# Even mixer of a two-layer hybrid backbone: a triangular solve with two VectorE operations a step, two products on VectorE in a round of their own, and loads issued one stage earlier

## The chip, the core and the metric

The kernel runs on one core of a Trainium2 chip. The metric is the device time of one execution, in microseconds (us); lower is better. The core has TensorE (PE in the profile, its weight loads PEld), VectorE (DVE), ScalarE (ACT), GpSimd (POOL) and SyncE (SP); every engine works through its own list of instructions in the order in which they were recorded, and waits on semaphores for the others. DMAs are issued from the lists of SP, ACT and POOL.

## The reference, cut to what matters

Two layers run over 256 context rows and 256 latent rows of width 1024. The first layer is "even": an RWKV-7 time mixing in both directions, beside a small pooling mixer; the second is "odd" (attention and retention). Each is followed by a mixture of gated MLPs, and every sub-layer adds its result to the residual stream `x` times a gate (`g1` after the mixer).

```python
def step(S, inp):                       # RWKV-7, per head; state S is (value, key)
    w_t, k_t, v_t, kk_t, b_t = inp[:5]
    sa = jnp.einsum('bhvk,bhk->bhv', S, -kk_t)
    S = S * w_t[:, :, None, :] + sa[..., None] * b_t[:, :, None, :] + v_t[..., None] * k_t[:, :, None, :]
    return S, jnp.einsum('bhvk,bhk->bhv', S, inp[5])
...
x = x + g1 * y_lat                      # y_lat: the mixer's output
```

## The kernel before

The scan is worked out in chunks of 64 tokens. Within a chunk, each token's correction depends on the earlier ones through a strictly triangular matrix (64 x 64 for each head and chunk), so the kernel inverts "one plus that matrix" for all chunks first and then walks over the chunks. The work is cut into four units, (half, d): half 0 or 1 is four of the eight heads, d 0 or 1 the direction. A unit has three parts:

- `ev_prep` makes the decays (EB, EN), the decayed keys KB, the receptances and keys times the decays (RK), their transposes (tok), and the chunk matrices: products of KB and RK, masked into BA (with the diagonal) and KK (without it).
- `ev_solve` inverts the 16 x 16 diagonal blocks row by row in 15 steps, and joins blocks with small matrix products (`products`, L819). A step spreads one row of the blocks over partitions by eight small matmuls into the bank "s" (L798); VectorE multiplies it with the rows found so far (L800), sums (L802), and negates and places the sum (L803). "s" has one buffer, so the matmuls of a step wait for the L800 of the step before. X is the inverse, A16 the blocks.
- `ev_chain` walks over the eight chunks, three rounds each, and reads KK, BA, RK and tok. Its first matmul (L864) needs what the solve wrote last.

The order of the work is set by `STAGES` (eight stages) and `weave`: in one round, every generator of the stage's main list is advanced by one `yield`, in order, and then `per` pieces of the fill list (projections of the inputs, "ada" pieces that turn the conditioning into gates) follow. What is recorded in that order is the order on each engine. In this text stages are numbered from 1: stage 3 holds prep (0,1), solve (0,0) and the bonus; 4 the chain (0,0) and the solve (0,1); 5 the chain (0,1) and prep (1,0); 6 the norm, the solve (1,0) and prep (1,1); 7 the solve (1,1), the chain (1,0), the bonus and the pooling; 8 the chain (1,1) and most of the output projection. After stage 8 comes the first mixture of MLPs.

All weights come through one `Stream`: SP issues the loads in the planned order, each as soon as a buffer of its ring is given back, and holds up there otherwise. In stage 8 `ev_first` loads the residual stream `x` again (into the tiles that held the projected inputs, hT) and the gate rows `g1` (into the tiles rT and us), with DMAs from ACT's list. Its L1521 multiplies a piece of the output by a piece of g1 (tiles us and rT), and L1522 adds it to x.

Of the kernel before, what the change touches and what calls it, by code (L numbers as in the profile page):

```python
# [32 lines left out]
def shape_constants():  # L33
# [49 lines left out]
    for d in range(2):  # L83
        after = (lambda a, b: a > b) if d == 0 else (lambda a, b: a < b)
        v[f"upto{d}"] = heads & ~after(p, f)
        v[f"strict{d}"] = after(f64, p % 64)
        v[f"incl{d}"] = ~after(p % 64, f64)
        v[f"start{d}"] = (p % 16 == f16) & (f16 == (0 if d == 0 else 15))
        v[f"cross{d}"] = (p % 32 // 16 == d) & (f32 // 16 == 1 - d)
# [6 lines left out]
    for i in range(16):  # L96
        v[f"sel{i}"] = (p % 32 // 16 == f32 // 16) & (p % 16 == i)
# [112 lines left out]
class Kernel:  # L210
# [182 lines left out]
    def even(self, xp, seg):  # L393

        nc, tc, I, c = self.nc, self.tc, self.I, self.c
        with ExitStack() as st:
# [6 lines left out]
                     (("BA", 4, 64), ("KK", 4, 64), ("RK0", 2, 64), ("RK1", 2, 64), ("tok0", 128), ("tok1", 128))]  # L403
# [3 lines left out]
            with ExitStack() as s1:  # L407
# [13 lines left out]
                for n in range(5):  # L421
# [255 lines left out]
    def ev_prep(self, half, d):  # L677
# [8 lines left out]
        u["BA"], u["KK"] = (up.tile([128, 8, 4, 64], F32, name=n) for n in ("BA", "KK"))  # L686
        u["Pe"], u["PH"] = up.tile([128, 2, 8], F32, name="Pe"), up.tile([128, 2, 8, 2], F32, name="PH")
        split = lambda a: a.rearrange("p (t j i) -> p t j i", t=4, j=2)
        for q in range(2):
# [50 lines left out]
            yield  # L740
            yield
# [24 lines left out]
    def ev_solve(self, half, d):  # L766
# [19 lines left out]

        A16 = wp.tile([128, G, 16], F32, name="A16")
# [1788 lines left out]
```

## Time and profile before

| what | us |
|---|---|
| median of 3 runs | 1911.77 |
| lowest and highest of them | 1896.86 and 1915.39 |
| the profiled execution, its own time | 1917.63 |
| span of the profiled execution | 1915.9 |

The profile is of one execution. Its span runs from the first instruction to the last, and 1.7 us lie around it. Busy times of PE include matmuls that run at either clock; PEclk is the granted share of TensorE's full clock, 1.00 being 2.4 GHz and 0.50 being 1.2 GHz. On the span's axis the even mixer lies from about 58 us (after the norm and the first projections) to 570 us, the first mixture from about 570 to 1080, the odd mixer to about 1330, and the second mixture to the end.

### The profile page before, as it was taken

The page shows a single profiled execution, that of the slowest core. Times are in us where ns is not written, and L with a number is a line of the kernel's source. Part 1 is how long each engine was busy: PE and PEld are TensorE (multiplying, and loading weights), DVE is VectorE, ACT ScalarE, POOL GpSimd, SP SyncE. Part 2 cuts the span into 40 slices and gives each one's busy share as a digit, 9 for nine tenths or more (in the row PEclk, how much of TensorE's full clock was granted, in tenths as well). Part 3 has the DMA queues.
Part 4 walks back from the last instruction along what each step waited for, and adds up shares of the span by engine and source line. Part 5 has one row for each costly group of instructions (what it writes and reads, how often), then busy time and mean ns, then how long its engine had stood idle before and what let it go on. Part 6 is the DMA issues. An engine that isn't in the chain of part 4 may idle for free. (4 is left out here: it accounts for less than half of the span.)

```text
span 1915.9 us, 31673 instructions
## 1 busy us (share of the span) xinstructions
PE 1653.2 (86%) x12946; PEld 931.2 (49%) x12946; DVE 842.5 (44%) x1718; ACT 435.9 (23%) x925; POOL 161.6 (8%) x181
## 2 busy tenths in 40 slices
PE   5987999889898999999999997999978787766666
PEld 3744556545676444444444435888643333422222
DVE  2556444655358245455555458563632212212012
ACT  3432122321213211111111114453421101101101
POOL 2122001112215000000000004000100000000000
PEclk8997888889998999999999998999888989979786
DMA  9266210461433879999999972422979998999991
GB/s 315 78 210 210 89 46 23 154 204 32 163 143 132 355 288 383 405 388 389 377 395 395 374 323 74 142 86 74 378 282 414 413 383 326 414 415 414 415 411 52
DMA packets 127284, 505.80 MB, mean 264 GB/s; under 512 B 11317, under 2 KB 38945, under 8 KB 85986
## 3 DMA queue, kind: packets, MB, share of 16 engines
q1 hardware_dynamic: 119794, 490.86, 66.0%
q0 software_dynamic: 3488, 8.26, 1.3%
q10 hardware_dynamic: 3792, 3.79, 0.6%
q8 instruction: 143, 2.34, 0.5%
q14 instruction: 67, 0.55, 0.1%
HBM read 501.78 MB, written 1.10 MB: 262 GB/s over the span
## 5 line engine op out<-in xcount | busy, mean ns | idle before, releaser
L1968 PE MATMUL b<-w,ht 128*64 128x512 f32 x512 | 118.8, 604 | 8.7 <-PEq L2185 8.5
L1993 DVE TENSOR_TENSOR tmp<-b,g 128x512 f32<-128x512 f32 x128 | 87.6, 686 | 70.1 <-PE b L1991 69.2
L1947 PE MATMUL b<-w,xg 128*64 128x512 f32 x512 | 116.9, 598 | 0.0
L1947 PE MATMUL b<-w,xh 128*64 128x512 f32 x512 | 116.9, 598 | 0.0
L2275 PE MATMUL b<-w,x 128*32 128x256 f32 x1024 | 80.4, 428 | 34.2 <-DMA w<-moe_w_up 28.4
L2292 PE MATMUL b<-w,ht 128*32 128x256 f32 x1024 | 79.8, 449 | 21.8 <-ACT ht L2287 12.7
L2275 PE MATMUL b<-w,xg 128*32 128x256 f32 x1024 | 76.8, 432 | 21.6 <-DMA w<-moe_w_up 13.3
L1995 DVE TENSOR_TENSOR x<-x,tmp 128x512 f32<-128x512 f32 x124 | 90.0, 726 | 4.3
L1976 DVE TENSOR_TENSOR yl<-b,yh 64x512 fp32r<-64x512 f32 x62 | 42.7, 689 | 101.6 <-ACT yh L1975 101.6
L2280 DVE SCALAR_TENSOR_TENSOR low<-b,gs,low 64x256 f32<-64x256 f32 x32 | 15.7, 491 | 158.5 <-ACT low L2279 158.5
L1968 PEld LDWEIGHTS b<-w,ht 128*64 128x64 f32 x512 | 41.5, 138 | 84.1 <-issue 70.8
L2440 DVE COPY y<-b 32x256 f32<-32x256 f32 x62 | 25.9, 418 | 127.5 <-PE b L2292 114.2
L1951 ACT ACTIVATE low<-b 64x512 f32<-64x512 f32 x33 | 19.4, 588 | 251.9 <-PEq L2185 221.3
L2275 PEld LDWEIGHTS b<-w,x 128*32 128x32 f32 x1024 | 37.0, 120 | 75.3 <-DMA w<-moe_w_up 37.9
L1952 DVE SCALAR_TENSOR_TENSOR low<-b,gs,low 64x512 f32<-64x512 f32 x32 | 36.1, 1130 | 67.0 <-ACT low L1951 64.2
L1975 ACT CAST yh<-b 64x512 fp32r<-64x512 f32 x62 | 36.0, 581 | 129.8 <-PE b L1968 106.5
L2275 PEld LDWEIGHTS b<-w,xg 128*32 128x32 f32 x1024 | 36.7, 123 | 58.7 <-DMA w<-moe_w_up 18.4
L1947 PEld LDWEIGHTS b<-w,xh 128*64 128x64 f32 x512 | 33.9, 136 | 62.5 <-issue 62.0
L1947 PEld LDWEIGHTS b<-w,xg 128*64 128x64 f32 x512 | 33.9, 136 | 62.3 <-issue 61.3
L2279 ACT ACTIVATE low<-b 64x256 f32<-64x256 f32 (+1 forms) x36 | 14.4, 399 | 214.6 <-PEq L2485 133.1
L1991 PE MATMUL b<-yh,oht 128*128 128x512 f32 (+1 forms) x128 | 58.3, 456 | 3.2 <-DVE tmp L1993 3.2
L2292 PEld LDWEIGHTS b<-w,ht 128*32 128x32 f32 x1024 | 34.5, 124 | 52.1 <-issue 20.2
(877 smaller groups left out, 3178.3 us busy)
## 6 DMA issues: line engine op xcount, KB each, us to landing
w<-moe_w_gate SPq DMA_DIRECT2D x128, 1024.0 KB
w<-moe_w_up SPq DMA_DIRECT2D x128, 1024.0 KB
w<-moe_w_down SPq DMA_DIRECT2D x128, 1024.0 KB
w<-ada_w SPq DMA_DIRECT2D x48, 1024.0 KB
w<-od_w_in SPq DMA_DIRECT2D x12, 1024.0 KB
w<-ev_w_in SPq DMA_DIRECT2D x8, 1024.0 KB
w<-ev_w_out SPq DMA_DIRECT2D x5, 1024.0 KB
w<-od_w_out SPq DMA_DIRECT2D x4, 1024.0 KB
```

What stands on the lines that cost most here:

```text
L1947: nc.tensor.matmul(ps[64 * j:64 * j + 64], xe(k), w[j][:, k % 4], start=k == 0, stop=k == 7)
L1951: nc.scalar.activation(sg[64:128], ps[0:64], AF.Silu)
L1952: nc.vector.scalar_tensor_tensor(hs[64:128].rearrange("s k q -> s q k"), ps[64:128].rearrange("s (q k) -> s q k", k=4), gs, sg[64:128].rea ...
L1968: nc.tensor.matmul(ps[64 * j:64 * j + 64], ht[:, k], w[:, k % 2, 512 * j:512 * j + 512], start=k == 0, stop=k == 3)
L1975: nc.scalar.copy(out=yh[:, j], in_=pj)
L1976: nc.vector.tensor_tensor(yl[:, j], pj, yh[:, j].bitcast(F32), op=ALU.subtract)
L1991: nc.tensor.matmul(ps, ohT[0:n, t], y[0:n, j], start=i == 0, stop=i == len(parts) - 1)
L1993: nc.vector.tensor_tensor(tmp, ps, g2[seg[t]][:, 512 * j:512 * j + 512], op=ALU.mult)
L1995: (nc.gpsimd if j in aside else nc.vector).tensor_tensor(xs, xs, tmp, op=ALU.add)
L2275: nc.tensor.matmul(ps[groups[j]], xe(k), w[j // 2][:, k % 4, 256 * (j % 2):256 * (j % 2) + 256], start=k == 0, stop=k == 7, skip_group_che ...
L2292: nc.tensor.matmul(ps[groups[j]], ht[:, k % 2, S * (k // 2):S * (k // 2) + S], w[:, k % 2, 256 * j:256 * j + 256], start=k == 0, stop=k == ...
L2440: (nc.scalar.copy if j % 2 else nc.vector.tensor_copy)(out=out, in_=ps[groups[j]])
```

## The change

It touches the even mixer alone.

1. **Solve.** A16 now holds minus the identity as well (`subtract` of eye16), and the `sel` constants are negated, so that the reduction writes the finished row straight into X: the third VectorE operation of a step (L803) is gone. The steps' matmuls cover one more column group (the diagonal), and are recorded for two steps at once into one bank; each step still has a `yield`. X starts from a copy by ScalarE. The masking of AT (L812) goes to ScalarE and GpSimd ahead of the steps, and half of the copy into TT to ScalarE. Four `yield`s with nothing in front of them are added: two ahead of the steps, one ahead of the first block product and one after the second.
2. **Prep.** BA and KK become the halves of one tile AB, masked by one operation on 128 x 512 elements where there were two on 128 x 256. The scaling of `th` goes from VectorE to ScalarE. The two products of RK go from GpSimd to VectorE, and into the next round.
3. **Loads.** g1 is loaded by SP in stage 7, in the pooling after the bonus, and `x` by SP in stage 7 after the last projection that reads hT; `ev_first` loads nothing.

```diff
@@ ev_prep
-        u["BA"], u["KK"] = (up.tile([128, 8, 4, 64], F32, name=n) for n in ("BA", "KK"))
+        both = up.tile([128, 8, 4, 128], F32, name="AB")
+        u["BA"], u["KK"] = both[:, :, :, 0:64], both[:, :, :, 64:128]
...
-            nc.vector.tensor_scalar(th, th, self.ka[:, 0, b:b + 1], self.ka[:, 1, b:b + 1], op0=ALU.mult, op1=ALU.add)
+            nc.scalar.activation(th, th, AF.Identity, bias=self.ka[:, 1, b:b + 1], scale=self.ka[:, 0, b:b + 1])
...
-            nc.gpsimd.tensor_tensor(u["RK"][q][:, :, 1], chunks(kk), eex, op=ALU.mult)
-            nc.gpsimd.tensor_tensor(u["RK"][q][:, :, 0], chunks(rT), ein, op=ALU.mult)
...
             yield
+            nc.vector.tensor_tensor(u["RK"][q][:, :, 1], chunks(kk), eex, op=ALU.mult)
+            nc.vector.tensor_tensor(u["RK"][q][:, :, 0], chunks(rT), ein, op=ALU.mult)
             yield
...
-                    nc.vector.tensor_tensor(u["KK"][:, C, 2 * q + h], ps[:, :, 64:128],
-                                            c[f"strict{d}"][:, None, :].to_broadcast([128, 4, 64]), op=ALU.mult)
-                    nc.vector.tensor_tensor(u["BA"][:, C, 2 * q + h], ps[:, :, 0:64],
-                                            c[f"incl{d}"][:, None, :].to_broadcast([128, 4, 64]), op=ALU.mult)
+                    nc.vector.tensor_tensor(both[:, C, 2 * q + h], ps, c[f"mask{d}"][:, None, :].to_broadcast([128, 4, 128]), op=ALU.mult)
@@ ev_solve
         yield
+        nc.scalar.activation(AT[:, :, 16 - 16 * d:32 - 16 * d], AT[:, :, 16 - 16 * d:32 - 16 * d], AF.Copy, scale=c["subcol"][:, d:d + 1])
+        nc.gpsimd.memset(AT[:, :, 16 * d:16 * d + 16], 0.0)
+        eye = c["eye16"][:, None, :].to_broadcast([128, G, 16])
         A16 = wp.tile([128, G, 16], F32, name="A16")
-        nc.vector.tensor_scalar(A16, A32[:, :, 0:16], c["subcol"][:, 0:1], None, op0=ALU.mult)
+        nc.vector.scalar_tensor_tensor(A16, A32[:, :, 0:16], c["subcol"][:, 0:1], eye, op0=ALU.mult, op1=ALU.subtract)
...
-        nc.vector.tensor_copy(X, c[f"start{d}"][:, None, :].to_broadcast([128, G, 16]))
-        for i in range(1, 16) if d == 0 else range(14, -1, -1):
-            r = slice(0, i) if d == 0 else slice(i + 1, 16)
...
-            nc.vector.tensor_tensor(tmp[:, :, 0:n], ps[:, :, 0:n], X[:, :, r], op=ALU.mult)
-            red = wp.tile([128, G], F32, name="red")
-            nc.vector.tensor_reduce(red, tmp[:, :, 0:n], axis=AX.X, op=ALU.add)
-            nc.vector.tensor_scalar(X[:, :, i], red, -1.0, c["eye16"][:, i:i + 1], op0=ALU.mult, op1=ALU.add)
-            yield
+        nc.scalar.copy(out=X, in_=eye)
+        yield
+        yield
+        rows = list(range(1, 16) if d == 0 else range(14, -1, -1))
+        while rows:
+            two, rows = rows[:2], rows[2:]
+            ps = pp.tile([128, 2, G, 16], F32, name="s")
+            span = lambda i: slice(0, i + 1) if d == 0 else slice(i, 16)
+            for j, i in enumerate(two):
...
+                    nc.tensor.matmul(ps[Q, j, :, 0:r.stop - r.start], c[f"sel{i}"][Q], A16[Q, :, r], start=j == 0, stop=i == two[-1],
+                                     skip_group_check=True)
+            for j, i in enumerate(two):
...
+                nc.vector.tensor_tensor(tmp[:, :, 0:n], ps[:, j, :, 0:n], X[:, :, r], op=ALU.mult)
+                nc.vector.tensor_reduce(X[:, :, i], tmp[:, :, 0:n], axis=AX.X, op=ALU.add)
+                yield
...
-        for s in range(2):
-            nc.vector.tensor_tensor(TT[:, :, 16 * s:16 * s + 16], X, sub[:, None, s, :].to_broadcast([128, G, 16]), op=ALU.mult)
+        nc.scalar.activation(TT[:, :, 16:32], X, AF.Copy, scale=c["subcol"][:, 1:2])
+        nc.vector.tensor_tensor(TT[:, :, 0:16], X, sub[:, None, 0, :].to_broadcast([128, G, 16]), op=ALU.mult)
         nc.vector.transpose(flat(TN), flat(TT))
-        nc.vector.tensor_tensor(AT, AT, c[f"cross{d}"][:, None, :].to_broadcast([128, G, 32]), op=ALU.mult)
+        yield
         yield
...
+        yield
         yield
@@ ev_u
+            if g == 3:
+                self.x = self.inputs(self.xp, nc.sync)
@@ ev_pool
+            if g == 0:
+                self.g1 = [[self.hp.tile([128, 512], F32, name=n) for n in ns] for ns in (("rT0", "rT1"), ("us0", "us1"))]
+                for j in range(2):
+                    for s in (1, 0):
...
+                        nc.sync.dma_start(out=self.g1[s][j], in_=self.mod[0][s:s + 1, a:a + 512].to_broadcast([128, 512]))
@@ ev_first
-        self.x = self.inputs(self.xp, nc.scalar)
-        self.g1 = [[hp.tile([128, 512], F32, name=n) for n in ns] for ns in (("rT0", "rT1"), ("us0", "us1"))]
```

On VectorE in stage 3, around the third and fourth steps of the solve (0,0), there stood before (line, operation, tile written and tiles read, shape; KB rows are prep's, sq the bonus's):

```order
L802 TENSOR_REDUCE red<-tmp 128x16
L803 TENSOR_SCALAR X<-red,const_heads 128x16
L723 SCALAR_TENSOR_TENSOR KB<-th,kk_437 128x4x128
L724 SCALAR_TENSOR_TENSOR KB<-KB,EN 128x4x128
L800 TENSOR_TENSOR tmp<-s,X 128x16x3
L802 TENSOR_REDUCE red<-tmp 128x16
L803 TENSOR_SCALAR X<-red,const_heads 128x16
L727 TENSOR_SCALAR th<-th,ka 128x512
L728 TENSOR_TENSOR KB<-th,kT_476 128x4x2x64
L729 TENSOR_TENSOR KB<-KB,EN 128x4x2x64
```

and there stands now, with line numbers of the changed kernel:

```order
L720 SCALAR_TENSOR_TENSOR KB<-th,kk_436 128x4x128
L721 SCALAR_TENSOR_TENSOR KB<-KB,EN 128x4x128
L808 TENSOR_TENSOR tmp<-s,X 128x16x2
L809 TENSOR_REDUCE X<-tmp 128x16
L725 TENSOR_TENSOR KB<-th,kT_475 128x4x2x64
L726 TENSOR_TENSOR KB<-KB,EN 128x4x2x64
L808 TENSOR_TENSOR tmp<-s,X 128x16x3
L809 TENSOR_REDUCE X<-tmp 128x16
L915 SCALAR_TENSOR_TENSOR sq<-rT_568,pc,kT_475 128x512
L916 TENSOR_TENSOR sq<-sq,us_686 128x512
L736 TENSOR_TENSOR RK_935<-kk_436,EB 128x8x64
L737 TENSOR_TENSOR RK_935<-rT_568,EB 128x8x64
```

The steps have two rows where they had three, the scaling of th has left the list, and the two RK products stand in a later round, after the bonus's two rows.

On PE from the end of the solve (0,0) to the end of stage 3 there stood before (f, c, C, p, P and s are PSUM banks; four L755 rows and then the chain's L864 follow):

```order
L819 MATMUL s<-TN,AT 32x32 x64
L283 MATMUL c<-const_ident,part 128x2 x4
L819 MATMUL s<-TT,A_1453 32x32 x64
L819 MATMUL s<-TN,KK 32x32 x32
L913 MATMUL C<-sq,const_heads 128x512
L746 MATMUL p<-const_ident,KB 128x128 x4
L819 MATMUL s<-TT,A_1566 32x32 x32
L746 MATMUL P<-const_ident,KB 128x128 x4
L755 MATMUL p<-RK_946,KB 128x128 x4
L755 MATMUL P<-RK_946,KB 128x128 x4
```

and there stands now, up to the chain's first row:

```order
L920 MATMUL C<-sq,const_heads 128x512
L743 MATMUL p<-const_ident,KB 128x128 x4
L825 MATMUL s<-TN,AT 32x32 x64
L743 MATMUL P<-const_ident,KB 128x128 x4
L825 MATMUL s<-TT,A_1420 32x32 x64
L752 MATMUL p<-RK_936,KB 128x128 x4
L752 MATMUL P<-RK_936,KB 128x128 x4
L825 MATMUL s<-TN,AB 32x32 x32
L752 MATMUL p<-RK_936,KB 128x128 x4
L825 MATMUL s<-TT,A_1542 32x32 x32
L752 MATMUL P<-RK_936,KB 128x128 x4
L871 MATMUL c<-VU_424,AB 64x64 x4
```

The block products stand further back, each with two other matmul groups or one between it and the next, and the last of them one group ahead of the chain where it was four.

The loads of x and g1 stood on ACT in stage 8, between the chain's copies:

```order
L877 ACTIVATE VU_426<-C 64x128
L478 DMA x_4455<-ctx 128x1024 x2
L478 DMA x_4456<-x 128x1024
L478 DMA x_4457<-x 128x1024
L1028 DMA rT_4462<-mod_76 128x512
L1028 DMA rT_4463<-mod_76 128x512
L1028 DMA us_4464<-mod_76 128x512
L1028 DMA us_4465<-mod_76 128x512
L869 COPY R<-C 128x128
```

and stand now on SP, among the weights of stages 7 and 8:

```order
L150 DMA w<-ada_w 128x4x512
L1019 DMA us_3733<-mod_76 128x512
L1019 DMA rT_3731<-mod_76 128x512
L1019 DMA us_3734<-mod_76 128x512
L1019 DMA rT_3732<-mod_76 128x512
L150 DMA w<-ada_w 128x4x512
L150 DMA w<-ev_w_out 128x8x256
L474 DMA x_3959<-ctx 128x1024 x2
L474 DMA x_3960<-x 128x1024
L474 DMA x_3961<-x 128x1024
L150 DMA w<-ev_w_out 128x8x256 x3
L150 DMA w<-ev_w_out 128x2x1024
```

They have changed lists, g1 ahead of the last "ada" weights and x behind the first tile of the output weights.

## Rows read from the trace of the kernel before

**Rows 1.** The page's 40 slices: granted clock in tenths, DMA share in tenths.
```profile
PEclk8997888889998999999999998999888989979786
DMA  9266210461433879999999972422979998999991
```

**Rows 2.** Windows about the stages 3 to 8, then most of the first mixture.
```profile
core 0: us, PE busy (x) PEld busy (x) DVE busy (x) ACT busy (x) POOL busy (x), PEclk, DMA share, GB/s
126.00:198.00 72.00, 58.15 (x854) 34.07 (x850) 43.43 (x102) 18.00 (x34) 16.22 (x23) 0.81 0.59 203
198.00:270.00 72.00, 69.47 (x935) 38.30 (x935) 36.97 (x105) 15.41 (x33) 0.00 (x0) 0.93 0.23 75
270.00:340.00 70.00, 63.71 (x472) 42.48 (x470) 27.50 (x63) 15.95 (x35) 7.92 (x10) 0.80 0.09 31
340.00:413.00 73.00, 62.99 (x883) 34.69 (x883) 45.69 (x104) 24.63 (x43) 13.66 (x15) 0.84 0.60 200
413.00:488.00 75.00, 71.18 (x945) 36.15 (x943) 40.69 (x105) 15.72 (x36) 17.44 (x29) 0.95 0.29 88
488.00:570.00 82.00, 75.16 (x574) 57.69 (x574) 33.66 (x79) 9.16 (x24) 9.16 (x16) 0.96 0.40 140
640.00:1080.00 440.00, 432.44 (x2162) 198.16 (x2162) 211.07 (x315) 79.55 (x148) 0.00 (x0) 1.00 0.94 374
```

**Rows 3.** Waits of PE in stage 3: us in total, times, longest.
```profile
PE s L798 <- DVE tmp L800: 5.4, 3, 4.3
PE s L819 <- DVE AT L812: 4.7, 1, 4.7
...
PE s L798 <- DVE A L789: 1.6, 1, 1.6
```

**Rows 4.** Timeline of DVE, 140 to 146: start us, us, instruction.
```profile
141.27 2.36 DVE L803 TENSOR_SCALAR X<-red,const_heads 128x16 f32<-128x16 f32 x1
144.10 0.69 DVE L728 TENSOR_TENSOR KB<-th,kT 128x512 f32<-128x512 f32 x1
144.83 1.63 DVE L729 TENSOR_TENSOR KB<-KB,EN 128x512 f32<-128x512 f32 x1
```

**Rows 5.** Timeline of POOL in the same stretch.
```profile
141.27 1.19 POOL L730 TENSOR_TENSOR RK<-kk,EB 128x512 f32<-128x512 f32 x1
142.41 1.17 POOL L731 TENSOR_TENSOR RK<-rT,EB 128x512 f32<-128x512 f32 x1
...
144.15 1.76 POOL L738 TENSOR_TENSOR us<-us,th 128x512 f32<-128x512 f32 x1 [0.44 <-DVE th L727]
```

**Rows 6.** Windows of 5 us around the stalls of stages 3 and 5.
```profile
150.00:155.00 5.00, 5.00 (x26) 1.32 (x28) 1.07 (x3) 0.58 (x1) 0.00 (x0) 0.50 0.12 26
320.00:325.00 5.00, 2.31 (x30) 1.77 (x26) 4.83 (x10) 0.27 (x1) 3.14 (x4) 0.75 0.00 0
340.00:345.00 5.00, 5.00 (x19) 2.48 (x18) 2.91 (x8) 1.83 (x3) 0.00 (x0) 0.50 0.00 0
```

**Rows 7.** Waits of PE, 318 to 326 (stage 5).
```profile
PE c L867 <- DVE ZB L890: 2.7, 1, 2.7
```

**Rows 8.** Timeline of PE, the end of stage 3.
```profile
172.89 0.61 PE L798 MATMUL s<-A,const_sel 32*32 32x240 f32 x8
...
197.97 0.27 PE L864 MATMUL c<-VU,KK 64*64 64x64 f32 x2
```

**Rows 9.** Timeline of ACT, 490 to 496: the last two g1 loads (ACTq is its list).
```profile
494.09 0.93 ACTq L1028 DMA_DIRECT2D us<-mod  x2
```

**Rows 10.** Timeline of DVE, 501 to 504; in brackets the idle time before.
```profile
502.10 0.42 DVE L1521 TENSOR_TENSOR th<-f,us 128x256 f32<-128x256 f32 x1 [8.59 <-DMA us<-mod]
```

**Rows 11.** Timeline of PE, 502 to 506.
```profile
503.24 0.48 PE L883 MATMUL C<-VU,tok 128*64 128x64 f32 x4 [5.16 <-DVE VU L878]
```

**Rows 12.** Groups of DVE, 58 to 570: count, busy us, mean ns, idle before.
```profile
L803 DVE TENSOR_SCALAR X<-red,const_heads 128x16 f32<-128x16 f32 x60 | 19.4, 324 | 2.1
...
L729 DVE TENSOR_TENSOR KB<-KB,EN 128x512 f32<-128x512 f32 x8 | 10.5, 1307 | 0.3
```

More of the change, by code (lines that the diff above doesn't have):

```diff
@@ L85, in shape_constants @@
         v[f"upto{d}"] = heads & ~after(p, f)
[L86 to L89, printed above, removed]
+        v[f"mask{d}"] = np.concatenate([~after(p % 64, f64), after(f64, p % 64)], axis=1)
     v["eye16"] = p % 16 == f16
@@ L96, in shape_constants @@
     for i in range(16):
-        v[f"sel{i}"] = (p % 32 // 16 == f32 // 16) & (p % 16 == i)
+        v[f"sel{i}"] = -1.0 * ((p % 32 // 16 == f32 // 16) & (p % 16 == i))
     n = np.arange(T_LAT)
@@ L402, in even @@
             parts = [self.up.tile([128, 8, *shape], F32R, name=n) for n, *shape in
-                     (("BA", 4, 64), ("KK", 4, 64), ("RK0", 2, 64), ("RK1", 2, 64), ("tok0", 128), ("tok1", 128))]
+                     (("AB", 8, 64), ("RK0", 2, 64), ("RK1", 2, 64), ("tok0", 128), ("tok1", 128))]
             parts = [a.rearrange("p a s i -> p (a s i)" if len(a.shape) == 4 else "p a i -> p (a i)") for a in parts]
@@ L429, in even @@
                         next(parameters)
-                        self.constants(mp, "even", ("heads", "upto0", "strict0", "incl0", "start0", "cross0", "upto1", "strict1", "incl1",
-                                                    "start1", "cross1", "eye16", "sub2", "subcol", "headsel", *(f"headrow{t}" for t in range(4))))
+                        self.constants(mp, "even", ("heads", "upto0", "mask0", "upto1", "mask1", "eye16", "sub2", "subcol", "headsel", *(f"headrow{t}" for t in range(4))))
                         self.constants(mp, "even", [f"sel{i}" for i in range(16)])
@@ L789, in ev_solve @@
         nc.vector.scalar_tensor_tensor(A16, A32[:, :, 16:32], c["subcol"][:, 1:2], A16, op0=ALU.mult, op1=ALU.add)
         X = wp.tile([128, G, 16], F32, name="X")
-        nc.vector.tensor_copy(X, c[f"start{d}"][:, None, :].to_broadcast([128, G, 16]))
-        for i in range(1, 16) if d == 0 else range(14, -1, -1):
-            r = slice(0, i) if d == 0 else slice(i + 1, 16)
-            n = r.stop - r.start
-            ps = pp.tile([128, G, 16], F32, name="s")
-            for k in range(4):
-                Q = slice(32 * k, 32 * k + 32)
-                nc.tensor.matmul(ps[Q, :, 0:n], c[f"sel{i}"][Q], A16[Q, :, r], start=True, stop=True, skip_group_check=True)
-            tmp = wp.tile([128, G, 16], F32, name="tmp")
-            nc.vector.tensor_tensor(tmp[:, :, 0:n], ps[:, :, 0:n], X[:, :, r], op=ALU.mult)
-            red = wp.tile([128, G], F32, name="red")
-            nc.vector.tensor_reduce(red, tmp[:, :, 0:n], axis=AX.X, op=ALU.add)
-            nc.vector.tensor_scalar(X[:, :, i], red, -1.0, c["eye16"][:, i:i + 1], op0=ALU.mult, op1=ALU.add)
-            yield
+        nc.scalar.copy(out=X, in_=eye)
@@ new lines, in ev_solve @@
+        yield
[6 more added lines that the diff above has]
+            for j, i in enumerate(two):
+                r = span(i)
+                for k in range(4):
+                    Q = slice(32 * k, 32 * k + 32)
+                    nc.tensor.matmul(ps[Q, j, :, 0:r.stop - r.start], c[f"sel{i}"][Q], A16[Q, :, r], start=j == 0, stop=i == two[-1],
+                                     skip_group_check=True)
+            for j, i in enumerate(two):
+                r = span(i)
+                n = r.stop - r.start
+                tmp = wp.tile([128, G, 16], F32, name="tmp")
+                nc.vector.tensor_tensor(tmp[:, :, 0:n], ps[:, j, :, 0:n], X[:, :, r], op=ALU.mult)
+                nc.vector.tensor_reduce(X[:, :, i], tmp[:, :, 0:n], axis=AX.X, op=ALU.add)
+                yield
@@ L1022, in ev_first @@
         nc, hp, pp = self.nc, self.hp, self.pp
-        self.x = self.inputs(self.xp, nc.scalar)
-        self.g1 = [[hp.tile([128, 512], F32, name=n) for n in ns] for ns in (("rT0", "rT1"), ("us0", "us1"))]
-        for s in range(2):
-            for j in range(2):
-                a = 2048 + 512 * j
-                nc.scalar.dma_start(out=self.g1[s][j], in_=self.mod[0][s:s + 1, a:a + 512].to_broadcast([128, 512]))
         for j in range(4):
```

1 line of the change is left out of this document (added).

## Prediction

> **What bounds the kernel now.** I read the slices first, to see whether time saved in the even mixer reaches the end. In slices 3 to 12, the mixer, the DMA share stands mostly at 0 to 6 tenths, so the weight stream waits for buffers; in the first mixture it is 9 [rows 1], but there PE is busy 432.44 of 440 us at a clock of 1.00 [rows 2], so PE sets that time. In slices 25 to 28 the stream stands at 2 to 4 tenths again, ahead of the second mixture, where it is 9. Each mixture starts from full buffers, so whatever the mixer saves should move all that follows.
>
> Then the stages [rows 2]. For each I take two losses: PE's idle time (length less busy), and the time lost to the lower clock (length times one less PEclk).
>
> | stage | idle | clock | both |
> |---|---|---|---|
> | 3 | 13.9 | 13.7 | 27.6 |
> | 4 | 2.5 | 5.0 | 7.5 |
> | 5 | 6.3 | 14.0 | 20.3 |
> | 6 | 10.0 | 11.7 | 21.7 |
> | 7 | 3.8 | 3.8 | 7.6 |
> | 8 | 6.8 | 3.3 | 10.1 |
>
> Together 95 us: a ceiling for what the mixer can give, not a forecast. The stages without a chain of chunks (3 and 6) lose most.
>
> Why PE idles is seen in its waits: in stage 3 it waits for VectorE, 5.4 us in three waits of the solve's matmuls, 4.7 us for the masking L812, 1.6 us for A16 [rows 3]. The longest, 4.3 us, is explained by the timelines: L803, an operation on 16 elements that takes 324 ns in the mean [rows 12], took 2.36 us from 141.27 [rows 4], exactly as long as GpSimd's two RK products, 1.19 and 1.17 us from the same moment [rows 5]. L729 took 1.63 us against 0.69 us for L728, which does as much, while GpSimd's 1.76 us sum on us ran [rows 4, 5]; over all eight, L729 averages 1307 ns [rows 12]. So VectorE stands still while GpSimd works on two inputs. What a stall costs besides itself is the clock: after that wait the granted clock is 0.50, and from 150 to 155 it still is, with PE busy throughout; after a wait of 2.7 us in stage 5 [rows 7] it is 0.75 between 320 and 325 and 0.50 as late as 340 to 345 [rows 6].
>
> **The change part by part.** The sum is made against the profiled execution, 1917.63 us, which is 5.9 us above the median of the runs.
>
> *The solve's third operation.* 60 times 324 ns is 19.4 us of VectorE [rows 12]. Little of it is on the path: the next matmuls depend on L800 (the bank), not on L803. It counts where VectorE is the late engine, stages 3 and 6.
>
> *RK on VectorE.* Eight pairs leave GpSimd, about 2.36 us a pair in which VectorE stood still, and VectorE gets two multiplications of 128 x 512, the size of L728: 2 x 0.69 = 1.4 us a pair. Even in plain VectorE time that is 1 us a pair to the good, and the 1.4 us fall in a round in which prep had nothing. In stage 5 the chain's round has them now; there they take the place of a wait of 2.7 us [rows 7].
>
> *th on ScalarE.* Between the two rounds of KB, VectorE now waits for ScalarE, and ScalarE for the first KB operation, which reads th. Behind VectorE's wait stand two KB products and the solve's next row; behind ScalarE's, in stage 5, the chain's copies. No row shows this handover; its bounds are 0 (ScalarE is done while VectorE sums a solve row) and 0.7 us each, about L728's length, for eight. I take 0.2, 2 us.
>
> *Stage 3.* The 4.3 us wait: VectorE has between two uses of bank s now KB (2 x 0.69), two solve rows, KB again (2 x 0.69, up to 1.63 for the second while the sum on us runs), but PE has two steps' matmuls and an "ada" piece ahead of its next use; about 1 us of wait is left, so 3.3 us, and the half clock to 155 or so, another 5. The 1.6 us for A16 goes with the two empty rounds. At the end, from the last step's matmul to the chain's first, 172.89 to 197.97 [rows 8], lie 25.1 us. By the new order L812 is gone from that path, but the bonus's two rows and RK stand ahead of TT, so a wait of some 3 us at the first block product stays, and the clock may fall once more; I count 19 to 21 us for the stretch: 5. In all 14, of 27.6. *Stage 6* has the same parts without the bonus, and the norm instead: 10, of 21.7.
>
> *Stages 4 and 7* begin with the solve's first matmul ahead of the chain's second on PE, waiting for A16; the empty rounds put it behind. I take 4 and 5 of 7.5 and 7.6. *Stage 5*: KB loses the standstill, so the chain's 2.7 us become about 1.2, and if the clock then holds, 10 us more; half of that with the first: 6.5.
>
> *Loads.* VectorE waits 8.59 us for g1 [rows 10], and PE 5.16 us behind it [rows 11]; the last g1 load was issued at 494 [rows 9]. Issued in stage 7 they are there. With part of the clock after it: 8.5. On SP the four loads of x wait for the last reading of hT, and behind them stand three tiles of output weights, which wait for PE at about that place too; at the rate of the first mixture, 374 GB/s [rows 2], 2 MB put those tiles back 5 us, and the second is first used a quarter of stage 8 (82 us [rows 2]) later: nothing. If that cover were gone, 5 us. The first prep (stage 2) is left at 0, with a bound of 3 for its two pairs.
>
> *What it costs.* A step's matmuls have 16 columns more; 240 take 0.61 us [rows 8], so at most 0.04 a step, 60 steps: 2. The solve ends four rounds later, and the chain follows the last block product with one group between: VectorE's and ScalarE's copies, 1 to 2.5 us at each of four ends, 6. Added work of ScalarE and the memsets of GpSimd: nobody waits for them in stages where ScalarE is busy 15 to 25 us of 70 [rows 2]; 0, up to 3.
>
> Sum: 14 + 10 + 4 + 5 + 6.5 + 8.5 = 48 less 2 + 2 + 6 = 10: 38 us. From 1917.6 that is 1880 us, and from the median 1874.
>
> The Trainium skill has a rule against half of this: "SBUF — State Buffer", section "Who interferes with whom", says that a VectorE instruction with two SBUF inputs and a GpSimd instruction that reads SBUF block each other wholly, and one with at most one such input does not contend. By that rule the RK products stay exposed on VectorE, and only the solve's two operations are free of GpSimd. If each of the six pairs in stages 3, 5 and 6 met a whole sum on us (the page's rule, the trace's 1.76 us), 11 us would go, and the sum would be 27. The trace agrees on the blocking of L729; that L803, with one tensor, was held too, it does not explain by this sentence alone.
>
> **The rivals.** (a) *Stalls and clock both go.* If no wait is long enough to bring the clock down, four fifths of the 95 us come, less 10: 66 us, 1846. For it: the clock is 1.00 wherever no long wait lies. Against: the ends of the solves still wait, and the chains have latencies of their own. 15%.
>
> (b) *Only the loads count.* PE's list stays as serial as it was: the waits move from the steps to the ends of the solve and the clock falls as often. Then 8.5 us and little more: 1903, within 1%. For it: the ends do get longer, and VectorE was not full in any stage (46 of 73 us at most [rows 2]). 16%.
>
> (c) *The ends of the solves decide.* The chain's first matmul waits for the copies at four ends; if each end has a wait of 1.5 us before the last product and 2.5 after it, and brings the clock down as the 2.7 us in stage 5 did, it costs 4 + 11 us, the latter half of the 22 us to 345 [rows 6, 7]: four are 60 against a gain of 48 less 4, so 16 us slower, 1928. It turns to a loss only with the third or fourth end (44 over 15). Against it: PE has other groups recorded between, and these waits should stay under the 2.7 us. 6%.
>
> That the change does nothing of what it says is ruled out by the order: the third row and the ACT loads are gone.
>
> **How the numbers follow.** My forecast, part of stalls and clock, has 63%, and lies from 1852 to 1895; predicted is 1874, 2.0% faster. About 1% (19 us) is what a measurement of this kernel tells from no change: its three runs lie 18.5 us apart. The range reaches into (a) and to the edge of (b): 1842 to 1903. Faster by over 1%, under 1893: nearly all of the forecast and (a), 77%; within 1%: (b), what is left of the forecast, and (c) as priced, 19%; slower by over 1%: (c) with longer waits, 4%.
>
> **What would show it.** In the changed profile: no operation of 16 elements above 0.5 us on VectorE in stages 3 and 6; KB's second product at 0.7 to 1.6 us; L1521 without a DMA wait; PE idle in stage 3 below 9 us and its PEclk above 0.87; stage 5 above 0.85. A wait of PE for AB or R at the chain's first two matmuls over 2.5 us with a clock of 0.50 behind would speak for (c). I am wrong if stages 3 and 6 are not shorter by at least 15 us together, or if a mixture after the mixer takes back what it gave.

## The result and the profile after

| what | us |
|---|---|
| changed kernel, median of 11 runs | 1888.95 (1877.45 to 1893.57) |
| kernel before, median of 11 runs | 1910.63 (1896.86 to 1916.64) |
| ratio, 95% interval | 0.9887 (0.9866 to 0.9907) |
| profiled execution of the changed kernel, time and span | 1889.25 and 1887.4 |

The change takes 21.7 us off, 1.1%. The forecast was 38 us: direction and range held, the size did not; 1888.95 lies near the slow end of the forecast's own span, 1852 to 1895. In the changed kernel the line numbers are its own: L802 are the solve's step matmuls (before L798), L825 the block products (L819), L920 the bonus's matmul (L913), L726 KB's second product (L729), L1530 the output times g1 (L1521).

The slices of the changed kernel's page answer to [rows 1]: in slices 3 to 12 the clock goes between 8 and 9 tenths, where it went between 7 and 9.

```profile
PEclk8998988989898999999999998999999889888887
DMA  9266300643144879999999981522889998999992
```

The same six stages in windows, each from the chain's or the step's matmul that begins it (columns as in [rows 2]):

```profile
126.00:192.50 66.50, 56.56 (x852) 33.86 (x848) 36.84 (x77) 20.41 (x39) 10.62 (x19) 0.84 0.64 221
192.50:262.00 69.50, 66.82 (x845) 36.28 (x846) 33.18 (x86) 15.10 (x34) 0.36 (x2) 0.97 0.28 90
262.00:330.00 68.00, 62.48 (x569) 43.30 (x565) 26.83 (x58) 19.13 (x39) 2.35 (x5) 0.80 0.06 19
330.00:400.60 70.60, 62.83 (x884) 36.86 (x884) 38.12 (x80) 26.93 (x48) 7.48 (x13) 0.84 0.63 210
400.60:478.00 77.40, 72.13 (x886) 37.22 (x886) 34.59 (x84) 16.65 (x39) 21.27 (x35) 0.92 0.42 136
478.00:556.00 78.00, 77.47 (x629) 59.80 (x630) 35.05 (x81) 9.79 (x25) 5.63 (x10) 0.95 0.28 96
```

VectorE and GpSimd are relieved as forecast (VectorE 43.43 to 36.84 us in stage 3, GpSimd 16.22 to 10.62). PE's clock hardly moves: 0.84 in stage 3, 0.80 in stage 5, and stage 7 has fallen from 0.95 to 0.92. To compare stages of all kernels alike, I read the start times of fixed matmuls from PE's timeline: the first of prep (0,0), the chain's first, the first of prep (1,0), the first step of the solves (1,0) and (1,1), the first and the last of the output projection. Between them lie, in us of one execution each:

```
kernel            2+3    4     5     6     7     8    sum
before           110.3  77.0  72.6  70.8  72.5  75.2  478.5
changed          103.0  74.6  73.3  67.8  73.8  69.8  462.3
e1_loads         110.3  77.5  72.3  69.1  71.2  68.1  468.5
e4_solve         103.4  74.6  73.7  65.6  72.4  75.4  465.0
e5_prep          104.4  77.1  64.3  67.8  71.2  76.0  460.8
e6_prep_loads    105.6  77.4  71.0  70.6  71.4  69.6  465.5
e3_x_late        101.6  74.8  73.6  67.8  73.1  70.2  461.0
e7_empty_d0      102.6  73.1  75.5  64.3  71.5  68.1  455.2
e10_ends_d0      103.3  70.0  77.0  65.4  74.9  69.2  459.8
e8_bonus          98.7  74.5  73.8  64.3  73.7  70.0  455.1
e11_rk_split      99.7  73.4  73.4  65.6  72.8  69.9  454.7
e14_rk_pool      102.1  74.6  73.4  65.9  72.7  69.7  458.4
e13_empty_bonus   99.6  74.9  77.7  62.1  71.2  68.1  453.6
e12_all           94.9  78.0  66.0  62.6  69.1  68.1  438.6
```

Kernels whose code is the same in a stage tell how far one execution can be trusted: mostly 2 to 3.5 us (stage 6 of the changed kernel and of e8_bonus: 67.8 and 64.3), once 7 (stage 5 of e5_prep and e6_prep_loads).

Two of these marks move with the change: where empty rounds stand ahead of a solve's steps, its first step comes two rounds later. By marks that stay (the first matmul of prep (1,1), between stages 5 and 6, and the first of the chain (1,0), between 6 and 7), stages 5, 6 and 7 take 65.1, 73.2 and 77.6 us before and 62.7, 70.8 and 81.4 after.

The stretch is 16.1 us shorter (it begins 1.9 us later on the changed kernel's span), and the lead is then kept: from the counting step of the first mixture (605.5 and 591.1 on the two spans) to that of the second (1388.4 and 1374.4) both kernels take the same.

```profile
605.50:1388.40 782.90, 748.07 (x4023) 427.27 (x4021) 412.88 (x749) 205.85 (x436) 39.82 (x37) 0.97 0.77 301
1388.40:1915.90 527.50, 376.23 (x3613) 174.43 (x3611) 119.83 (x281) 67.52 (x179) 6.95 (x8) 0.85 0.89 358
```

```profile
591.10:1374.40 783.30, 747.24 (x4021) 427.23 (x4020) 412.90 (x747) 205.52 (x435) 38.90 (x36) 0.98 0.77 300
1374.40:1887.40 513.00, 361.61 (x3613) 169.03 (x3611) 120.03 (x283) 68.23 (x179) 7.84 (x8) 0.88 0.91 370
```

The first fence is of the kernel before, the second of the changed one. The rest, 14.5 us of the difference between the two profiled executions, lies in the second mixture, which the change does not touch; counted alike, e7_empty_d0 took 523.9 us there and e8_bonus 516.0. So I put the mixer's gain at some 16 us. Whether any of the 5.6 us between that and the medians is owed to the change stays open.

### The profile page after: what moved, and what is told of

Read it like the earlier page. It is cut to its first block, busy times and chain, and to the rows that moved or that the text cites. A ratio compares the mean times of both kernels' runs of the same rounds, so it can differ in the third digit from the quotient of the medians.

```text
span 1887.4 us, 31596 instructions
## 1 busy us (share of the span) xinstructions
PE 1636.5 (87%) x12946; PEld 930.7 (49%) x12946; DVE 817.7 (43%) x1622; ACT 446.9 (24%) x945; POOL 139.3 (7%) x169
## 3 DMA queue, kind: packets, MB, share of 16 engines
q8 instruction: 144, 2.36, 0.5%
## 5 line engine op out<-in xcount | busy, mean ns | idle before, releaser
L2284 PE MATMUL b<-w,xg 128*32 128x256 f32 x1024 | 73.7, 412 | 22.5 <-DMA w<-moe_w_up 13.6
L1374 PE MATMUL b<-w,hH 128*128 128x256 f32 x320 | 60.9, 291 | 0.0
```

The costliest lines, as they stand in the source:

```text
L1374: nc.tensor.matmul(ps[:, t], l[:, k, T], r[:, k], start=t == 0 and k == 0 and i == 0, stop=k == 7 and i == 2, skip_group_check=True)
L2284: nc.tensor.matmul(ps[groups[j]], xe(k), w[j // 2][:, k % 4, 256 * (j % 2):256 * (j % 2) + 256], start=k == 0, stop=k == 7, skip_group_che ...
```

## The experiments

Ratios are to the kernel before, run beside each group of experiments on the same chip; a gain in us is worked out from the ratio.

**Each part alone.** e1_loads adds only the loads to the kernel before, e4_solve only `ev_solve` and the negated `sel`, e5_prep only `ev_prep` with the tile AB; the edits are those pieces of the diff.

> The kernel before with the early loads alone (g1 in the pooling, x after the last reading of hT, both on SP). The forecast has 8.5 us for them: about 1902, ratio 0.9955. Theory T1 (blocks of PE's instructions come late while the weights load at 350 to 400 GB/s; in the changed kernel PE stands 3.7 us in the block products at the end of stage 7, with a clock of 0.50 behind): the 8.59 us wait of VectorE goes, but a standstill of PE marked as issue, 2 to 4 us, comes at the end of stage 7, and half a clock behind it, so 0 to 4 us gain, ratio 0.998 to 1.000. Theory T2 (the loads are worth their forecast, and the solve or the prep was sized too high): ratio 0.9955, no such standstill over 1 us.

Measured: 1899.64 us, ratio 0.9959 (0.9935 to 0.9983), which is 7.8 us of the 1908.82 that the kernel before took beside it, and stage 8 is 7.1 us shorter. The loads are worth their forecast when they stand alone, without a standstill at the end of stage 7. T2 holds here.

> The kernel before with the solve part alone (two operations a step, masking of AT on ScalarE and GpSimd, four empty rounds). The forecast's terms that belong to it: some 6.6 us of stage 3's 14, 5 of stage 6's 10, 4 and 5 in stages 4 and 7, less 2 for wider matmuls and 6 for the ends of the solves: 12.6 us, ratio 0.9934. T1 gives less, 3 to 8 us (0.996 to 0.9985), with standstills marked as issue at the block products of stages 3 and 6, where the weights load at over 200 GB/s. T2, if the solve is the part that was sized too high: the same total without these standstills, with waits for TN, A or AB in their place.

Measured: 1902.05 us, 0.9973 (0.9951 to 0.9994): 5 us of the 12.6. Stages 2 and 3 are shorter by 6.9 us and stage 6 by 5.2, as forecast; stage 4 gives 2.4, and stage 7 is 2.4 us longer by the marks that stay (80.0 us), for a forecast 9. The total is T1's, the places are not: PE stands 1.35 us in a block product of stage 6 and in none of stage 3, but 3.39 us at the end of stage 7, at 339 GB/s, without the early loads. The profiled execution, 1893.46 us, was the fastest of the twelve, so these stages show more than the median gained.

> The kernel before with the prep part alone (one masking operation on AB, th on ScalarE, RK on VectorE in a round of its own). The forecast's terms that belong to it: some 8 us of stage 3's 14, 5 of stage 6's 10, 6.5 in stage 5, less 2 for the handover of th: 17.5 us, ratio 0.991. T1 says nothing against this. T2, if prep is the part that was sized too high: 5 to 10 us, 0.995 to 0.997, with KB's second product still at 1.3 us or more beside the sum on us.

Measured: 1897.9 us, 0.9943 (0.992 to 0.9967): 11 us of the 17.5. Stages 2 and 3 give 5.9, for a forecast 8. KB's second product averages 918 ns, not T2's 1.3 us. Its stage 5 was 8.3 us shorter in the profiled execution, but e6_prep_loads, with the same code there, has 1.6.

**What the parts do to each other.**

> The changed kernel with x loaded from ACT in stage 8, as in the kernel before; g1 stays early. T1: the standstill of PE at the end of stage 7 falls below 1 us, the granted clock from there to 20 us on is above 0.8, and the time is 5 to 9 us under the changed kernel's: ratio 0.984 to 0.986 to the kernel before. T2: as the changed kernel, 0.987 to 0.990, or slower if x is now late for the first pieces of the output.

```diff
@@ ev_u
-            if g == 3:
-                self.x = self.inputs(self.xp, nc.sync)
@@ ev_first
+        self.x = self.inputs(self.xp, nc.scalar)
```

Measured: 1888.89 us, 0.9894 (0.9876 to 0.9913), the changed kernel's time. T1's blame of x falls: PE still stands 3.33 us in the block product, while output weights come in at 344 GB/s over those 5 us:

```profile
466.44 0.50 PE L825 MATMUL s<-TT,A 32*32 32x32 f32 x35 [3.33 <-issue]
...
462.00:467.00 5.00, 1.67 (x136) 1.42 (x134) 3.03 (x5) 0.58 (x1) 1.50 (x2) 1.00 1.03 344
```

> The kernel before with the prep part and the early loads, without the solve part. The runs so far: from the first matmul of the first prep to the last of the output projection, the kernel before takes 478.5 us, the loads alone 468.5, prep alone 460.8, the solve part alone 465.0, and the changed kernel 462.3: alone they take 10, 17.7 and 13.4 us off, together only 16.1. Theory T3 (the solve part's empty rounds put the ends of the solves of stages 4 and 7 behind the chain's last round, and take back there what prep and the loads gave): without the solve part the two add up, some 452 us for that stretch, and the time is 4 to 8 us under the changed kernel's, ratio 0.983 to 0.987. Theory T4 (prep and the loads spoil one another, whatever the solve does, for instance over PE's instruction blocks): 458 to 462 us and 0.988 to 0.991.

Measured: 1887.11 us, 0.9893 (0.9865 to 0.9921), and 465.5 us for the stretch. T3's figure of 452 us was not reached; it leaned on the short stage 5 of e5_prep. The ratio is T4's, but the run times do not show that prep and loads spoil one another: alone they take 10.9 and 7.8 us off, together 20.4. With the solve part's 5.2 us the three parts alone come to 24 us and the changed kernel to 21.6, each with an interval of 4 to 5 us either way. So the parts add up within what the runs can tell, and fall short alone: 24 us of the 38.6 expected of them. Whether the solve part adds anything beside the other two, these runs can't tell.

**The empty rounds.**

> The changed kernel with the four empty rounds only in the solves of stages 3 and 6 (d = 0), none in the solves of stages 4 and 7, which run beside a chain of 24 rounds. T3: the stretch of stages 4 and 5 falls by about 6 us and that of 7 and 8 by about 4; 2 to 4 us come back as waits for A16 at the first steps: 4 to 8 us under the changed kernel, ratio 0.984 to 0.987. T4: no gain, or 2 to 4 us slower by the waits for A16, 0.989 to 0.991.

```diff
         nc.scalar.copy(out=X, in_=eye)
-        yield
-        yield
+        if d == 0:
+            yield
+            yield
...
         nc.vector.transpose(flat(TN), flat(TT))
-        yield
+        if d == 0:
+            yield
         yield
```

(and the same ahead of the third block product). Measured: 1876.56 us, 0.9847 (0.9812 to 0.9883), by the ratios some 8 us under the changed kernel. The two intervals touch, but the three kernels without these rounds in stages 4 and 7 (this one, e13_empty_bonus, e12_all) have 0.981 to 0.9847, and the changed kernel and the five others made from it 0.9880 to 0.9923. The stretch is 7.1 us shorter: by the marks that stay, 4.7 us in stage 7 (76.7) and 1.7 in stage 8, where T3 expected 4, and 1.7 in stages 4 and 5 together, where it expected 6; stage 6 is 1.3 longer. The waits of PE from 400 to 480, the whole of stage 7, are now:

```profile
PE s L803 <- DVE A L788: 2.7, 1, 2.7
PE C L886 <- ACT R L879: 1.7, 1, 1.7
PE C L877 <- DVE ZB L900: 0.2, 1, 0.2
```

The wait for A16 came back, as expected, and the standstill in the block product went: both large products now lie ahead of the burst of weights.

```profile
453.00:458.00 5.00, 5.00 (x213) 3.03 (x213) 1.76 (x5) 0.59 (x1) 0.00 (x0) 1.00 0.01 3
458.00:463.00 5.00, 5.00 (x132) 3.01 (x119) 1.40 (x2) 2.37 (x5) 1.10 (x2) 1.00 0.08 20
463.00:468.00 5.00, 5.00 (x160) 3.09 (x153) 1.83 (x4) 2.95 (x6) 4.22 (x4) 1.00 0.90 266
```

> The changed kernel with the two empty rounds ahead of the steps kept everywhere, and the two at the block products only in the solves of stages 3 and 6. T3: part of what the removal of all four gives (the last product comes two rounds earlier, not four), without the waits for A16: 3 to 7 us under the changed kernel, 0.985 to 0.987. T4: as the changed kernel, 0.988 to 0.990.

The edit is that of e7_empty_d0 without its first piece. Measured: 1887.96 us, 0.988 (0.9847 to 0.9913), as the changed kernel. The waits for A16 are gone, but the second block product, two rounds later than in e7_empty_d0, meets the burst: 3.80 us of standstill in stage 7.

**The bonus and RK.**

> The changed kernel with two more empty rounds in the bonus, between its two products on VectorE and its matmul. In the changed kernel's stage 3 PE waits 3.7 us at that matmul, which stands ahead of the first block product, and the granted clock is 0.5 to 0.7 from 170 to 195. If that wait is what is left of stage 3's loss: it goes, the clock of that stretch is above 0.8, and 5 to 8 us are gained, ratio 0.985 to 0.986. Rival: the wait moves to the block product itself (TN comes a little later than sq), the clock falls as before, and the time stays, 0.988 to 0.990.

```diff
             nc.vector.tensor_tensor(sq, sq, us, op=ALU.mult)
             yield
             yield
+            yield
+            yield
```

Measured: 1886.88 us, 0.9905 (0.9874 to 0.9936). The rival was right about the wait (it moved to the block product, 4.0 us for TN), but stages 2 and 3 are 4.3 us shorter in the trace; the medians don't tell it from the changed kernel.

> The changed kernel with the two RK products on VectorE in two rounds, one in each of the rounds in which prep has nothing else. In the changed kernel's stage 5 PE waits 1.4 us for the chain's VU, which stands behind both products on VectorE, and the granted clock falls to 0.50 for some 15 us behind it. Theory T5 (this wait decides whether the clock falls): it becomes 0.7 us or less, the clock behind it stays above 0.65, stage 5 falls from 73 us to 65 to 68, and the time is 5 to 8 us under the changed kernel's, ratio 0.984 to 0.986. Rival: the chain's other waits there (1.1 and 1.2 us, for a copy behind ScalarE's exponentials and for ZB behind KB) are enough for the fall: stage 5 stays at 72 to 75 us, ratio 0.987 to 0.990.

```diff
             nc.vector.tensor_tensor(u["RK"][q][:, :, 1], chunks(kk), eex, op=ALU.mult)
+            yield
             nc.vector.tensor_tensor(u["RK"][q][:, :, 0], chunks(rT), ein, op=ALU.mult)
             yield
-            yield
```

Measured: 1890.92 us, 0.9906 (0.9872 to 0.9939). The 1.37 us wait for VU went, the waits of 1.09 and 1.18 us stayed, and the clock fell all the same: the rival holds.

> The changed kernel with the two RK products back on GpSimd, in the round in which VectorE has them now. The forecast's theory (VectorE stands still beside a GpSimd operation of two inputs, so the products cost VectorE more from there than on itself): operations of VectorE in that round take 1 us or more too long, stages 3 and 6 lose 2 to 3 us each, stage 5 loses nothing or gains 1; ratio 0.989 to 0.992. Rival: in a round of their own they meet little of VectorE's work, VectorE is 1.4 us freer in each, PE's wait for VU in stage 5 goes: as fast as the changed kernel or faster, 0.984 to 0.988.

```diff
-            nc.vector.tensor_tensor(u["RK"][q][:, :, 1], chunks(kk), eex, op=ALU.mult)
-            nc.vector.tensor_tensor(u["RK"][q][:, :, 0], chunks(rT), ein, op=ALU.mult)
+            nc.gpsimd.tensor_tensor(u["RK"][q][:, :, 1], chunks(kk), eex, op=ALU.mult)
+            nc.gpsimd.tensor_tensor(u["RK"][q][:, :, 0], chunks(rT), ein, op=ALU.mult)
```

Measured: 1893.82 us, 0.9923 (0.9898 to 0.9947), just past the slow end of what the forecast's theory gave, and its interval overlaps the changed kernel's. The losses of 2 to 3 us in stages 3 and 6 are not in its trace (102.1 with stage 2, 65.9 in stage 6; the stretch is 458.4), and PE's wait for VU in stage 5, which the rival had go, is 0.98 us. The cost to VectorE is seen in single operations. The longest of the eight L726 (the others take 0.98 to 2.83 us) lasts as long as GpSimd's sum on us and both RK products behind it:

```profile
135.98 4.18 DVE L726 TENSOR_TENSOR KB<-KB,EN 128x512 f32<-128x512 f32 x1
...
136.09 1.27 POOL L733 TENSOR_TENSOR us<-us,th 128x512 f32<-128x512 f32 x1
137.31 1.17 POOL L736 TENSOR_TENSOR RK<-kk,EB 128x512 f32<-128x512 f32 x1
138.44 1.17 POOL L737 TENSOR_TENSOR RK<-rT,EB 128x512 f32<-128x512 f32 x1
```

The Trainium skill ("SBUF — State Buffer", section "Who interferes with whom") has two such operations block each other wholly; the trace agrees: 1.27 + 1.17 + 1.17 is 3.61 us, and in the changed kernel L726 alone takes 0.69 where GpSimd is idle. Here the operation that is recorded first, L726, by 0.11 us, is the one that is held.

**Together.**

> The changed kernel with the empty rounds only in the solves of stages 3 and 6, and the bonus two rounds later as a whole (its products on VectorE and its matmul), so that in stage 3 TT and TN stand ahead of it on VectorE and the first block product on PE. Without the late bonus this kernel took 1876.6 us. Theory: the 3.7 us wait at the end of stage 3 is sq's place on VectorE and goes now: stages 2 and 3 fall by 3 to 6 us, 1871 to 1875 us, ratio 0.981 to 0.9835. Rival: PE waits as long for TN, which needs the last row of the solve: as without it, 0.9835 to 0.985.

In the bonus the two new `yield`s stand ahead of the products on VectorE; the rest is e7_empty_d0. Measured: 1879.81 us, 0.9847 (0.9808 to 0.9885). PE's wait at the end of stage 3 is 2.19 us for TN where it was 3.71 for sq, and stages 2 and 3 are 3 us shorter than in e7_empty_d0; the medians do not show it.

> The changed kernel with all three edits: empty rounds only in the solves of stages 3 and 6, the bonus two rounds later, and the RK products in two rounds. If T5 and the theory of the bonus hold, 1866 to 1872 us, ratio 0.977 to 0.981, the fastest of all. Rival: the clock's falls are only moved from one place to another, 1873 to 1880, as the kernel with the fewer empty rounds alone.

The edits of e13_empty_bonus and e11_rk_split. Measured: 1870.52 us, 0.981 (0.9775 to 0.9845), the fastest, clear of the changed kernel's interval and by the ratios some 15 us under it, with 438.6 us for the stretch. All stages but 4 are at or near their shortest, and stage 5, which e11_rk_split left at 73.4, is 66.0.

## Why the forecast was too high

The mechanisms that it named are there. L1530 has no DMA wait left (L1521's 8.59 us in [rows 10]), no 16-element operation of VectorE exceeds 0.42 us (L803's 2.36 in [rows 4]), and KB's second product averages 1074 ns (1307 in [rows 12]). But PE still idles 9.9 us in stage 3, not under 9, and its clock is 0.84 there and 0.80 in stage 5, where signs of 0.87 and 0.85 were named. The sizes of four terms failed, those of stages 7, 6, 3 and 5. In the table below, "stretch" goes by the marks of the table of stages, the last column by the marks that stay.

| term | forecast | stretch | marks that stay |
|---|---|---|---|
| stages 2 and 3 | 14 | 7.3 | 7.3 |
| stage 4 | 4 | 2.4 | 2.4 |
| stage 5 | 6.5 | -0.7 | 2.4 |
| stage 6 | 10 | 3.0 | 2.4 |
| stage 7 | 5 | -1.3 | -3.8 |
| stage 8 (loads) | 8.5 | 5.4 | 5.4 |
| costs | -10 | inside the above | inside the above |
| sum | 38 | 16.1 | 16.1 |

Two sums of the prediction are off in themselves. The parts named for stage 3 (3.3, 5, 1.6 and 5) make 14.9, not 14. And only four of its six RK pairs could meet a sum on us: in stage 5 GpSimd copies us (L735, 1.13 us) and sums nothing, so 7 us, not 11, would go by that rule. The section of the Trainium skill that is cited there ("SBUF — State Buffer", "Who interferes with whom") also sets a condition that the prediction leaves out: an operation with at most one SBUF input does not contend outside the two-port modes, and tensor_scalar, which L803 is, is among those that can enter them. So the 2.36 us of L803 do not speak against that section; whether L803 ran in such a mode no trace here shows.

*Stage 7, the step "the empty rounds put it behind".* They did, and the A16 wait of 3.6 us went. I counted what four later rounds cost at the chain's end, but not where the block products would land. Before, PE was busy throughout that place, beside DMAs of 7 GB/s (the wait for A16, the second product, and its window):

```profile
PE s L798 <- DVE A L789: 3.6, 1, 3.6
...
473.82 1.29 PE L819 MATMUL s<-TT,A 32*32 32x32 f32 x128
...
471.00:476.00 5.00, 5.00 (x200) 3.37 (x186) 1.76 (x6) 0.71 (x2) 0.00 (x0) 1.00 0.03 7
```

Now the second product runs into the burst of weights and stands, marked as issue:

```profile
463.66 0.99 PE L825 MATMUL s<-TT,A 32*32 32x32 f32 x93
468.38 0.50 PE L825 MATMUL s<-TT,A 32*32 32x32 f32 x35 [3.73 <-issue]
```

and the clock falls behind it (windows, columns as in [rows 2]; the share of the DMA engines and GB/s are the last two):

```profile
460.00:465.00 5.00, 4.64 (x253) 2.82 (x246) 2.73 (x4) 1.60 (x4) 4.45 (x4) 1.00 0.89 291
465.00:470.00 5.00, 1.62 (x47) 1.18 (x46) 2.60 (x5) 0.30 (x1) 0.12 (x1) 0.88 1.02 399
470.00:475.00 5.00, 5.00 (x41) 2.73 (x41) 0.66 (x2) 1.87 (x6) 2.15 (x3) 0.50 1.09 350
475.00:480.00 5.00, 4.31 (x138) 4.00 (x134) 0.04 (x1) 3.71 (x6) 2.32 (x5) 0.50 0.35 74
480.00:485.00 5.00, 4.47 (x24) 3.08 (x26) 1.63 (x3) 1.25 (x4) 0.00 (x0) 0.50 0.01 3
```

That e7_empty_d0, which moves these products forward again, has neither the standstill nor the low clock shows that the rounds were the cause. All fourteen kernels agree: by the marks that stay, stage 7 takes 80.0 to 82.5 us in the seven whose solve (1,1) has empty rounds, each with a standstill of 3.3 to 3.8 us there, and 73.1 to 77.6 in the seven others, which have none. The last product also trails the chain: it begins at 477.99, behind the chain's last chunk at 468.81, where before it stood ahead of that chunk (481.53 and 484.32). Part of stage 8's missing 3 us lies here too: it begins at half clock, and is 68.1 in e1_loads and in e7_empty_d0. In *stage 6* a standstill of the same kind grew from 1.94 to 3.40 us, with a clock of 0.50 for 17 us behind it. In e8_bonus, e11_rk_split and e14_rk_pool, with the same solve there, the low clock is shorter (7 to 10 us), and the stage takes 68.6 to 68.9 by the marks that stay, so the 10 would be some 4.5 there; e10_ends_d0 has 72.2.

*Stage 3, "a wait of some 3 us at the first block product stays".* It did, as 3.71 us at the bonus's matmul ahead of that product; the timelines show why: sq and RK stand ahead of TT on VectorE, and sq behind L726, which met the sum on us.

```profile
169.97 1.64 DVE L726 TENSOR_TENSOR KB<-KB,EN 128x512 f32<-128x512 f32 x1
...
173.52 0.69 DVE L916 TENSOR_TENSOR sq<-sq,us 128x512 f32<-128x512 f32 x1 [0.47 <-DVE sq L915]
...
174.27 2.07 PE L920 MATMUL C<-sq,const_heads 128*128 128x512 f32 x2 [3.71 <-DVE sq L916]
```

What I mis-sized is the clock behind it: 0.55 still from 185 to 190. The stretch from the last step's matmul to the chain's first took 168.94 to 192.53, 23.6 us, not 19 to 21. In stages 2 and 3 the solve part alone gives 6.9 us, the prep part alone 5.9, and both together 7.0 to 8.7 (the changed kernel, e3_x_late, e7_empty_d0, e10_ends_d0). Up to the last step's matmul the two nearly add up: from prep's first matmul it takes 85.3 us before, 82.9 with the solve part, 79.6 with prep, 76.6 to 79.5 with both. It is the end that is lost. Alone, the solve part brings it from 25.1 to 20.5 us, inside the forecast's 19 to 21, and prep leaves it at 24.8; together they take 23.6 to 25.0. So the prep part takes back there what the solve part gave. That it does so by its rows ahead of TT on VectorE is argued from the order: with RK off VectorE (e14_rk_pool) the end takes 22.5, with the bonus's matmul later (e8_bonus) 21.8, one execution each.

*Stage 5, "if the clock then holds, 10 us more; half of that".* The wait for ZB fell from 2.7 to 1.18 us, as forecast. But the RK products, now on VectorE, put a new wait of 1.37 us for VU behind it, in the same few us:

```profile
310.40 0.65 PE L890 MATMUL C<-VU,tok 128*64 128x64 f32 x6 [1.09 <-ACT VU L884]
...
312.96 0.44 PE L874 MATMUL c<-ZB,RK 128*64 128x128 f32 x4 [1.18 <-DVE ZB L897]
...
316.43 0.48 PE L890 MATMUL c<-VU,tok 128*64 128x64 f32 x4 [1.37 <-DVE VU L885]
```

I had named the place and taken it for an exchange. That this wait decides is ruled out by e11_rk_split, where it is gone and the clock stays low as long. The condition "if the clock then holds" was never met: the clock fell to 0.50 at these waits in all 14 profiled executions. It stayed there for 20 to 31 us in twelve (24 before, 20.5 in the changed kernel) and for 7 us in two (e5_prep, e12_all), whose stage 5 was 7 to 9 us shorter than the changed kernel's. Half of the 10 us was too much for a short fall that came in two of 14.

Rival (b) took the loads for the only thing that counts; e6_prep_loads and e12_all speak against it. Rival (c)'s price per end was near (a standstill of 3.73 us and 17 us of half clock), but only at the ends in stages 7 and 6, of which only stage 7's is new, and not by the copies it named: PE waits at most 1.3 us for A or R there. My own test, stages 3 and 6 shorter by 15 us together, failed: with stage 2 they give 10.3.

## What to carry to other kernels

An empty round in a generator that ends last in its stage makes the stage longer: count the rounds of each before adding one, and look at what the DMA queues do where the late work will land. (No run took the empty rounds out of stages 3 and 6, so what they cost there is open.) Size the end of a stage with the order that all parts of a change leave there; one part can take back there what another gave. Where a low clock stands behind a wait, cost it as a short or a long one, each with a chance, not as half.

## What the runs showed of the hardware

**PE stands still in groups of many small matmuls, longer beside the weights.** In the block products (128 matmuls of 32 columns in some 1.3 us) PE stood still with nothing to wait for, in every kernel. Taking the DMA rate over the standstill and the microsecond ahead of it: at 0 to 28 GB/s it lasts 0.2 to 2.0 us, at 64 to 210 GB/s 1.4 to 2.3, and at 279 to 414 GB/s 2.2 to 3.8. From 464 to 469 in the changed kernel, this row of the queues (packets, MB, share of 16 engines) stands beside the weights:

```profile
q8 instruction: 1, 0.02, 1.4%
```

A packet of this instruction queue falls into every standstill over 2 us. That PE waits for it is argued from this and from the rates; no run took the packet alone away, and four standstills of 1.15 to 1.50 us in block products (e3_x_late, e8_bonus, e11_rk_split, e14_rk_pool) have none, so it is not the whole cause. The Trainium skill ("Runtime: NRT & Kernel Launch", section "Instruction fetch mechanics") calls the cost of crossing a block of instructions "mostly hidden"; if the packet is what PE waits for, it was 3.73 us here, and the low clock behind it.

**The same waits, a long and a short low clock.** e11_rk_split and e12_all have the same three waits in stage 5 (1.09, 1.18 or 1.19, and 0.37 us). Windows of the first, then of the second:

```profile
304.20:311.20 7.00, 4.35 (x50) 3.25 (x50) 5.23 (x12) 2.70 (x6) 0.88 (x2) 0.71 0.00 0
311.20:318.20 7.00, 7.00 (x53) 5.61 (x53) 1.90 (x5) 1.71 (x4) 0.00 (x0) 0.50 0.01 2
318.20:325.20 7.00, 7.00 (x40) 6.38 (x40) 2.56 (x4) 1.07 (x2) 0.00 (x0) 0.50 0.00 0
325.20:331.00 5.80, 5.80 (x18) 2.39 (x18) 2.69 (x8) 1.83 (x3) 0.52 (x2) 0.50 0.22 69
```

```profile
304.50:311.50 7.00, 4.35 (x48) 3.33 (x48) 5.53 (x13) 2.37 (x6) 0.88 (x2) 0.73 0.00 0
311.50:318.50 7.00, 7.00 (x74) 5.68 (x73) 2.30 (x6) 2.63 (x6) 0.00 (x0) 0.78 0.01 2
318.50:325.50 7.00, 6.77 (x45) 3.32 (x41) 5.61 (x12) 3.01 (x7) 0.51 (x2) 1.00 0.23 71
308.00:314.00 6.00, 5.46 (x46) 4.22 (x46) 4.53 (x10) 1.13 (x4) 0.69 (x1) 0.50 0.00 0
```

PE is busy 4.35 us of the first seven in both, and 7.00 of the next seven. The clock falls to 0.50 in both: in the first for 24 us, to 331, in the second for 7 us, from 308 (the last row) to 314.5. What decides it these runs do not tell, so how much of e12_all's 15 us comes of its edits, and how much of a low clock that happened to be short in its runs, is open too.
